# The delta-rule phase of a hybrid block with TensorE's order formed in the source, decays kept in SBUF and one inverse

## The chip, the cores and the metric

The kernel runs on one core of one Trainium2 chip. The metric is the device time of one execution in microseconds (us); of several runs the median counts. Engines are named as in the profile: PE (TensorE; its weight loads are PEld), DVE (VectorE), ACT (ScalarE), POOL (GpSimd) and SP (SyncE, which here only issues DMAs).

## The reference

One layer for 512 tokens of width 1024, float32. Two mixers read the same normalised input through one wide projection `w_in`: a gated delta rule (8 heads, keys of 128, values of 256) and a retention (4 heads of 256 and 512). Their gated outputs pass `w_br`, are mixed, pass `w_out`, and a squared-ReLU MLP follows. The change is in the delta rule, here as the reference has it:

```python
qkv = silu(causal_depthwise_conv(concatenate([qa, ka, va]), conv_a))
qa = l2norm(qa) * A_DK ** -0.5
ka = l2norm(ka)
beta, g = sigmoid(beta_logit), -exp(a_log) * softplus(a_dt + dt_bias)
# in chunks, per head
g_cum = cumsum(g)
decay = exp(where(causal, g_cum[:, None] - g_cum[None, :], -inf))
lower = where(strict, (k * beta) @ k.T * decay, 0)
t_inv = inverse(I + lower)                      # unit lower triangular
u, w = t_inv @ (v * beta), t_inv @ (k * beta * exp(g_cum))
attn = where(causal, q @ k.T * decay, 0)
for each chunk:
    v_new = u - w @ state
    o = (q * exp(g_cum)) @ state + attn @ v_new
    state = state * exp(g_last) + (k * exp(g_last - g_cum)).T @ v_new
oa = rmsnorm(o, norm_a) * silu(za)
```

The reference works in chunks of 64. Both kernels take chunks of 128, four per head, which gives the same sums in another grouping.

## The kernel before

Tokens lie in four tiles of 128, features in tiles of 128. Every weight passes through `weights` (lines 88 to 103): one DMA of 512 KB on SP's queue into one of two buffers `raw`, then a split into a rounded part `whi` (ACT, line 117) and the rest `wlo` (DVE, line 118), three buffers each. Every product is three float32r matmuls, hi x hi, hi x lo and lo x hi: `mm3` (lines 81 to 86), called by `feature_major` and `token_major`. One weight tile feeds 24 matmuls of 512 columns. Results stand in PSUM: four banks `mm` for projections, three `dl` and one `tr` for everything else. Small products and transposes inside the delta rule are plain float32 matmuls.

The stages in time: the start (normalisation, transposition of the input, the first key projection; to about 45 us), the delta rule (to about 430 us), the retention with its products of blocks (`seven`, with block sums that POOL's queue adds in DRAM), the mix, and the MLP.

The order of instructions on each engine comes from a scheduler that reads the program in source order, with priorities: `tc.high_priority(n)` moves a block n places ahead, `tc.keep_in_program_order` fixes an instruction against the others so marked, and `tc.issue_after(x)` puts instructions behind `x` on its own engine. Before, almost all of the delta rule's matmuls were left to the scheduler.

The delta rule before, for groups of four heads (`g4`) and pairs of heads (`g2`):

- `keys` (683): projection, `conv_silu` (630: copy to `c_raw` with a margin of three, one scaled copy on ACT, three multiply-adds on DVE, Tanh on ACT, one closing multiply on DVE, line 646), transposition into `kd`, sums of squares, `rsqrt`. Then per head `decays` and a matrix `mt` of scaled key products (713), and a scaling of `kd` (716).
- `decays` (659): for one head, eight copies of the triangle `tri`, scaled by the two parts of `g` (665, ACT), two matmuls of the constant `later` on them (666), and Exp (668). It is called once per head in `keys` and again in `values_queries`.
- `base_inverse` (720), called for each `g4`: the diagonal blocks of 32x32 of 16 matrices go to DRAM and come back as 64 rows (POOL's queue); 31 elimination steps of two DVE operations each (741, 747); the result goes back through DRAM into `rt` and, for `double_blocks`, into `rn`.
- `double_blocks` (758), four calls of eight matrices: blocks of 32 become blocks of 64 and 128 through four rounds of small matmuls (780, 786/789, 797, 801).
- `values_queries` (804): projections and convolutions of values and queries of a pair, and the masked query-key products `at`.
- `recurrence` (846): per chunk the products with the state (862, 894), with the inverse (871), the state's update (880) and the output (901), with DVE and ACT steps between.
- `gated` (927) projects `za`, and `gate_rows` (600) takes Tanh (604), completes silu (605) and multiplies the rows (607). `gated_features` (609) transposes and splits them into `og`; `ya_partial` (671) multiplies them by `w_br`.

The calls stand at lines 932 to 954; the state of one pair is worked on while the next pair's projections run. Query buffers `qf` are two.

Of the kernel before, what the change touches and what calls it, by code (L numbers as in the profile page):

```python
# [10 lines left out]
F32 = mybir.dt.float32  # L11
# [8 lines left out]
P = 128  # L20
# [7 lines left out]
OFF_GA, OFF_GBR = 12304, 13328  # L28
DFF = 4096


def shape_constants():
# [3 lines left out]
    later = (j[:, None] > j[None, :]).astype(np.float32)  # L36
    c_mat = np.concatenate([ident, tri, later], axis=1)
# [23 lines left out]
def hybrid_block_kernel(ctx: ExitStack, tc: tile.TileContext, a: dict, out: bass.AP):  # L61
# [11 lines left out]
    later_copies = [24]  # L73
    marks = []
# [13 lines left out]
    def weights(src, k0, nk, c0, ncols, keep=None, paced=True):  # L88
# [11 lines left out]
        with ExitStack() as behind:  # L100
            for mark in marks if i < 9 else ():
                behind.enter_context(tc.issue_after(mark.ins))
            return split_weights(raw, n, nk, keep, 200 if i >= 6 else 0)
# [207 lines left out]
    cmat = cp.tile([P, 3 * P], F32, name="cmat")  # L311
# [4 lines left out]
    later = cp.tile([P, P], F32R, name="later")  # L316
# [14 lines left out]
    ghi = cp.tile([P, 4, 8], F32, name="ghi")  # L331
    glo = cp.tile([P, 4, 8], F32, name="glo")
# [30 lines left out]
    rk = pa.tile([P, 32], F32, name="rk")  # L363
    rinv = pa.tile([P, 32], F32, name="rinv")
    br = pa.tile([P, 32], F32, name="br")
    nc.gpsimd.memset(rt, 0.0)

    with tc.tile_pool(name="xp", bufs=2) as xp:
# [64 lines left out]
        def to_features(t, xn, pss):  # L433
            for k in range(8):
                transpose(pss[k % 4][:, k // 4, t % 2 * P : t % 2 * P + P], xn[:, k * P : (k + 1) * P])
# [59 lines left out]
        with tc.issue_after(later_in.ins):  # L495
            nc.gpsimd.dma_start(cmat[:, P : 3 * P], a["c_mat"][:, P : 3 * P])
# [25 lines left out]
        def small_half(th):  # L522
            ts = slice(256 * th, 256 * th + 256)
            for i in range(16):
                nc.tensor.matmul(
                    pba[0:32, ts], ba_w[:, i % 8, 0:32], xs[i // 8][:, i % 8, ts],
                    start=th + i == 0, stop=i == 15, skip_group_check=True,
                )

        pba = psx.tile([P, T], F32, tag="tr", name="pba", bufs=1)  # L530
        small_half(0)
        to_features(2, xn2, pss)
        to_features(3, xn3, pss)
        for k in range(8):
            features(1, k, pss, marks.append)
        small_half(1)
        pv = psx.tile([P, 4, P], F32, tag="dl", name="tr", bufs=3)
        transpose(pv[:, 0, :], vecs_in)
        nc.vector.tensor_copy(vecs, pv[:, 0, 0:18])
        transpose(pv[:, 1, :], conv_in)  # L540
        nc.vector.tensor_scalar(convw, pv[:, 1, :], 0.5, None, ALU.mult)
        with tc.issue_after(marks[-2].ins):
            nc.scalar.copy(later, cmat[:, 2 * P : 3 * P])
# [4 lines left out]
    baT = pa2.tile([32, T], F32, tag="st", name="baT", bufs=2)  # L548
    for i in range(2):
        nc.scalar.copy(baT[:, i * 256 : i * 256 + 256], pba[0:32, i * 256 : i * 256 + 256])  # L550
    pb = psx.tile([P, 4, P], F32, tag="tr", name="tr", bufs=1)
    for c in range(4):
        nc.tensor.transpose(pb[:, c, 0:32], baT[:, c * P : (c + 1) * P], ident[0:32, 0:32])
    scratch = pa2.tile([P, T], F32, tag="vn", name="scratch")
    ba = scratch[:, 0:64].rearrange("p (c h) -> p c h", c=4)

    def small(i):
        return scratch[:, 64 + 32 * i : 96 + 32 * i].rearrange("p (c h) -> p c h", c=4)

    both = scratch[:, 272:400].rearrange("p (c h) -> p c h", c=4)  # L560
    nc.vector.tensor_copy(both, pb[:, :, 0:32])
    nc.vector.tensor_tensor(ba, both[:, :, 0:16], both[:, :, 16:32], ALU.add)
    nc.scalar.activation(beta, ba[:, :, 0:8], AF.Exp, scale=-1.0)
    nc.vector.tensor_scalar(beta, beta, 1.0, None, ALU.add)
    nc.vector.reciprocal(beta, beta)
    z, e, u, lnu, um1, g = (small(i) for i in range(6))
    dt_b = ab[:, 8:16].unsqueeze(1).to_broadcast([P, 4, 8])
    nc.vector.tensor_tensor(z, ba[:, :, 8:16], dt_b, ALU.add)
    nc.vector.scalar_tensor_tensor(e, z, -1.0, z, ALU.mult, ALU.max)
    nc.scalar.activation(e, e, AF.Exp, scale=-1.0)  # L570
    nc.vector.tensor_scalar(u, e, 1.0, None, ALU.add)
    nc.scalar.activation(lnu, u, AF.Ln)
    nc.vector.scalar_tensor_tensor(um1, u, -1.0, e, ALU.add, ALU.subtract)
# [847 lines left out]
```

## Time and profile before

| what | value |
|---|---|
| runs, median of 3 (lowest to highest) | 1362.84 us (1362.74 to 1366.62) |
| span of the profiled execution | 1362.5 us |
| what the median of the runs has over that span | 0.3 us |
| instructions in the span | 17876 |
| granted TensorE clock, mean | 0.999 |
| POOL busy, share of the span | 109.4 us, 8% |
| data moved by DMA | 214.70 MB, mean 158 GB/s |

A row of an engine or of a group gives busy time as the union of its instructions' durations, their count, the mean duration of one in ns, and the idle time of the engine just ahead of them with what ended it. Matmuls overlap, so their durations are longer than the distance between their starts. A row of the windows gives the stretch and its length, then for each engine the busy time and, in brackets, the count, and at the end the granted clock, the share of the DMA engines and GB/s. A row of the waits reads: engine and line that waited, what released it, total us, number of times, longest. A row of the timeline begins with the start in us and the duration of the instruction, or of several alike.

### The profile page before, as it was taken

How to read it: one execution, taken by the hardware profiler on the slowest of the kernel's cores; microseconds unless marked ns; L12 is line 12 of the kernel's file. 1: busy time of each engine (PE TensorE's matmuls, PEld its weight loads, DVE VectorE, ACT ScalarE, POOL GpSimd, SP SyncE). 2: the span in 40 equal slices, each digit the busy share in tenths (PEclk: the TensorE clock that was granted, in tenths of full speed). 3: DMA queues.
4: the chain of work that ended last, by engine and by line, in shares of the span. 5: the costliest groups of instructions: out<-in, count | busy, mean ns of one | idle time of the engine just before them, and what ended most of it. 6: DMA issues, size and time to landing. Idle time of an engine off the chain costs nothing.

```text
span 1362.5 us, 17876 instructions
## 1 busy us (share of the span) xinstructions
PE 1347.0 (99%) x6685; PEld 1110.7 (82%) x6685; DVE 912.8 (67%) x1606; ACT 651.7 (48%) x1204; POOL 109.4 (8%) x161
## 2 busy tenths in 40 slices
PE   9999999999999999999999999999999999999997
PEld 7888787788877888888888888888889888888886
DVE  5799899864665557567477577575775744828535
ACT  5977564624543322453453343343355736436441
POOL 2010310121011002000000100011101100000000
PEclk9999999999999999999999999999999999999999
DMA  5254715379458447775584782488639843625421
GB/s 178 64 154 133 202 43 180 117 153 238 108 124 169 110 147 158 190 240 193 131 255 132 192 263 93 154 217 182 199 117 238 224 154 110 197 95 169 132 86 62
DMA packets 101718, 214.70 MB, mean 158 GB/s; under 512 B 7158, under 2 KB 20624, under 8 KB 101120
## 3 DMA queue, kind: packets, MB, share of 16 engines
q1 hardware_dynamic: 85616, 170.41, 39.1%
q0 software_dynamic: 15280, 42.03, 17.0%
q8 instruction: 52, 0.85, 0.3%
q10 hardware_dynamic: 736, 1.12, 0.2%
q14 instruction: 34, 0.28, 0.1%
HBM read 207.77 MB, written 64.49 MB: 200 GB/s over the span
## 4 chain that ended last, share of the span: by engine, by line
PE 89%; DVE 5%; DMA 2%; ACT 2%; issue 1%; DVEq 0%; ACTq 0%
PE mm L84 18%; PE mm L85 18%; PE mm L86 18%; PE mm L242 10%; PE dl L242 10%; PE tr L323 3%; PE mm L456 2%; DVE wlo L118 1%; PE dl L86 1%; PE dl L85 1%; PE dl L84 1%; PE dl L901 1%; PE dl L871 1%; DVE c_y L642 1%; PE dl L880 1%; PE dl L862 1%
## 5 line engine op out<-in xcount | busy, mean ns | idle before, releaser
L118 DVE TENSOR_TENSOR wlo<-raw,whi 128x1024 fp32r<-128x1024 f32 x245 | 298.8, 1221 | 269.0 <-ACT whi L117 267.7
L117 ACT CAST whi<-raw 128x1024 fp32r<-128x1024 f32 x245 | 257.4, 1052 | 428.9 <-PE mm L85 243.4
L84 PE MATMUL mm<-actT,whi 128*128 128x512 f32 x480 | 190.1, 396 | 0.0
L85 PE MATMUL mm<-actT,whi 128*128 128x512 f32 x480 | 189.9, 396 | 0.0
L86 PE MATMUL mm<-actT,wlo 128*128 128x512 f32 x480 | 189.0, 395 | 0.0
L84 PEld LDWEIGHTS mm<-actT,whi 128*128 128x128 f32 x480 | 90.2, 188 | 18.7 <-ACT c_y L640 0.8
L86 PE MATMUL mm<-hn,wlo 128*128 128x512 f32 (+1 forms) x288 | 105.4, 366 | 0.0
L85 PE MATMUL mm<-hn,whi 128*128 128x512 f32 (+1 forms) x288 | 105.3, 366 | 0.0
L84 PE MATMUL mm<-hn,whi 128*128 128x512 f32 (+1 forms) x288 | 105.3, 366 | 0.0
L86 PEld LDWEIGHTS mm<-actT,wlo 128*128 128x128 f32 x480 | 90.3, 188 | 17.9
L85 PEld LDWEIGHTS mm<-actT,whi 128*128 128x128 f32 x480 | 90.3, 188 | 17.8
L84 PE MATMUL mm<-og,whi 128*128 128x512 f32 x256 | 99.7, 390 | 1.0 <-DVE zz L605 1.0
L85 PE MATMUL mm<-og,whi 128*128 128x512 f32 x256 | 99.6, 389 | 0.0
L86 PE MATMUL mm<-og,wlo 128*128 128x512 f32 x256 | 99.6, 389 | 0.0
L242 PE MATMUL mm<-whi,xsum 128*128 128x512 f32 x256 | 80.8, 389 | 0.0
L642 DVE SCALAR_TENSOR_TENSOR c_y<-c_raw,convw,c_y 128x512 f32<-128x512 f32 x96 | 69.7, 743 | 2.4 <-ACT c_y L640 1.8
L85 PEld LDWEIGHTS mm<-hn,whi 128*128 128x128 f32 x288 | 54.3, 189 | 8.8
L84 PEld LDWEIGHTS mm<-hn,whi 128*128 128x128 f32 x288 | 54.3, 189 | 8.7
L86 PEld LDWEIGHTS mm<-hn,wlo 128*128 128x128 f32 x288 | 54.3, 189 | 8.7
L84 PE MATMUL mm<-whi,actT 128*128 128x512 f32 x152 | 61.1, 402 | 0.1
L242 PE MATMUL dl<-whi,actT 128*128 128x512 f32 x192 | 61.1, 389 | 0.0
L242 PE MATMUL dl<-whi,ffq 128*128 128x512 f32 x192 | 61.0, 389 | 0.0
(345 smaller groups left out, 2608.8 us busy)
## 6 DMA issues: line engine op xcount, KB each, us to landing
raw<-in_w_in_dram SPq DMA_DIRECT2D x101, 512.0 KB, 4.3
raw<-sums SPq DMA_DIRECT2D x56, 512.0 KB, 4.2
raw<-in_w_up_dram SPq DMA_DIRECT2D x36, 512.0 KB, 4.6
sums<-in_w_in_dram SPq DMA_DIRECT2D x32, 512.0 KB, 5.6
sums<-sums POOLq DMA_DIRECT2D x28, 512.0 KB, 7.1
raw<-in_w_down_dram SPq DMA_DIRECT2D x26, 512.0 KB, 3.8
sums<-in_w_down_dram SPq DMA_DIRECT2D x24, 512.0 KB, 7.4
raw<-in_w_br_a_dram SPq DMA_DIRECT2D x16, 512.0 KB, 4.0
```

What stands on the lines that cost most here:

```text
L84: nc.tensor.matmul(ps, lh, rh, start=first, stop=False)
L85: nc.tensor.matmul(ps, lh, rl, start=False, stop=False)
L86: nc.tensor.matmul(ps, ll, rh, start=False, stop=last)
L117: nc.scalar.copy(hi[:, :n], raw[:, :n])
L118: nc.vector.tensor_tensor(lo[:, :n], raw[:, :n], hi[:, :n], ALU.subtract)
L242: m = nc.tensor.matmul(pss[t], lhs[i // 2], rhs[i % 2], start=first and k + i == 0, stop=k + i == 5, skip_group_check=not first,)
L323: nc.tensor.transpose(ps, src, ident)
L456: nc.tensor.matmul(ps[:, ts], ws[w][:, kk, f * P : (f + 1) * P], xs[x][:, k, ts], start=first and kk + i == 0, stop=kk == len(ks) - 1 and ...
L642: nc.vector.scalar_tensor_tensor(y, raw[:, j : j + T], tap(j), y, ALU.mult, ALU.add)
L862: nc.tensor.matmul(ks[:, hh, :], kf[:, h0 + hh, cs], state[:, hh, :], start=True, stop=True)
L871: nc.tensor.matmul(px[:, hh, :], rt[:, nn[hh], :], vx[:, hh, :], start=True, stop=True)
L880: nc.tensor.matmul(pc[:, hh, :], kd[:, nn[hh], :], vn[:, hh, :], start=True, stop=True)
```

## The change

Outside the delta rule two things change: the gate of the retention is one Silu on ACT instead of Tanh and a DVE operation, and a scaling of its `rstd` goes. The constant `later` and its load go. At the start, the transposes of tokens 256 to 511 are interleaved by feature pairs, and half of the second half of the first key product is put ahead of the small projection's second half, all fixed in program order.

The delta rule is written anew:

- **Order.** A class `Clock` runs while the kernel is written, not on the chip. It holds a model of PE's time; each matmul and transpose of the phase goes through it and is fixed in program order. Work is of two kinds. *Chains* (keys, inverse, doubling, recurrence, gates) yield planned delays or names of events. *Fillers* (projections, in pieces of some microseconds) run when no chain is due. Projections for keys, values, queries and `w_br` are cut into pieces of 256 columns, holding two `mm` banks.
- **Decays.** Row sums of `g` go to DRAM once, come back broadcast over the partitions, are masked on POOL, and 32 Exps on ACT with a per-partition bias leave all decays in `dall` (32 x 128 columns of SBUF). The query products are multiplied into the same place.
- **Scalings.** `kd` is not scaled any more; the products with the inverse are copied twice on ACT, with `brd` (decay to the chunk's end included) for the state and with `br` for the output.
- **Convolution.** The three multiply-adds read PSUM, without the copy; Silu on ACT closes it for values and queries (Tanh and a DVE operation still for keys, since every Silu is put behind the last Exp).
- **Inverse.** One `base_inverse` for all 32 matrices on 128 partitions. DVE's own 32x32 transposes take the place of the trips through DRAM. Each operation of a step is cut in two halves. `double_blocks` runs its four rounds over all four groups.
- **Query buffers.** `qf`, `ssq` and `rq` have three buffers, so that the third pair's queries need not wait for the first pair.
- **Gates.** `za` passes Silu straight from PSUM; one DVE multiplication per tile and head follows.

The delays and the lists, as the source has them (lines of the diff, cut):

```diff
+SMALL_US, CONV_US, TOK_US, PK_US, INV_US, DB_US = 10.5, 6.5, 2.5, 2.0, 62.0, 0.5
+VT_US, KS_US, PX_US, PC_US, GATE_US, FEAT_US, INV_PRIO, CONV_PRIO, SMALL_PRIO, KEY_PRIO, DECAY_US, AHEAD, TR_US = 2.5, 2.4, 3.5, 2.4, 11.0, 1.0, 0, 600, 800, 600, 20.0, 700, 2.2
...
+        def run(self, fillers):
...
+                due = [c for c in self.chains if self.ready(c[0]) <= self.now]
+                if due:
+                    self.step(min(due, key=lambda c: self.ready(c[0])))
+                    continue
+                if current is None:
+                    for f in fillers:
+                        if all(self.events.get(n, float("inf")) <= self.now for n in f[1]):
+                            fillers.remove(f)
+                            current = f[0]()
+                            break
...
+            gb = pa2.tile([P, 16, P], F32, tag="vt", name="gb", bufs=2)
+            rows = g_d[16 * g4 : 16 * g4 + 16].rearrange("n t -> (n t)")
+            nc.gpsimd.dma_start(gb.rearrange("p n t -> p (n t)"), rows.partition_broadcast(P))
+            nc.gpsimd.affine_select(
+                gb, gb, pattern=[[0, 16], [1, P]], compare_op=ALU.is_ge, fill=-1e30, base=0, channel_multiplier=-1
+            )
...
+                        nc.scalar.activation(
+                            dall[:, 4 * h + c, :], gb[:, 4 * i + c, :], AF.Exp, bias=neg_g[:, c, h : h + 1]
+                        )
...
-        for j in (2, 1, 0):
-            nc.vector.scalar_tensor_tensor(y, raw[:, j : j + T], tap(j), y, ALU.mult, ALU.add)
-        nc.scalar.activation(th, y, AF.Tanh)
-        nc.vector.scalar_tensor_tensor(dst, th, 1.0, y, ALU.add, ALU.mult)
+            for j in (2, 1, 0):
+                s = 3 - j
+                nc.vector.scalar_tensor_tensor(y[:, s:T], ps[:, 0 : T - s], tap(j), y[:, s:T], ALU.mult, ALU.add)
+            if th is None:
+                with tc.issue_after(exps[-1].ins):
+                    nc.scalar.activation(y, y, AF.Silu, scale=2.0)
...
+                for bs in blocks:
+                    nc.vector.transpose(
+                        mb[bs].rearrange("p (c m) -> p c m", m=32), mt[bs, :, bs].rearrange("p n c -> p c n")
+                    )
+                for j in range(31):
...
+                    cuts = (0, (nr + 1) // 2, nr) if nr > 3 else (0, nr)
...
+            clock.done("inverse", INV_US)
...
+                    qs = chain_bank()
+                    for hh in range(2):
+                        clock.matmul(qs[:, hs[hh], :], qf[:, hh, cs], state[:, hs[hh], :], start=True, stop=True)
+                    yield KS_US - (clock.now - t1)
...
+                    for w, scale in ((vx, brd), (vn, br))[c == 3 :]:
+                        for hh in range(2):
+                            nc.scalar.activation(w[:, hs[hh], :], px[:, hs[hh], :], AF.Copy, scale=scale[:, nn[hh] : nn[hh] + 1])
+                yield PX_US
...
+        clock.run(
+            [
+                (second_keys_filler, ()),
+                (value_filler(0), ()),
+                (query_filler(0), ()),
+                (gate_filler(0), ()),
+                (value_filler(1), ()),
+                (query_filler(1), ()),
+                (ya_filler(0), ("og0", "doubled")),
+                (value_filler(2), ("og0",)),
+                (query_filler(2), ()),
+                (gate_filler(1), ("gate0",)),
+                (ya_filler(1), ("og1",)),
+                (value_filler(3), ("og1",)),
+                (query_filler(3), ("og1",)),
+                (gate_filler(2), ("gate1",)),
+                (ya_filler(2), ("og2",)),
+                (gate_filler(3), ("gate2",)),
+            ]
+        )
```

801 lines of the change are left out of this document (493 added, 308 removed).

## The prediction, written before the result

> **What bounds the kernel now.** I read the page's first lines, then the busy time of each engine by stage (the windows: length, then busy us and count of PE, PEld, DVE, ACT, POOL, then the granted clock), then what PE waited for.
>
> ```profile
> span 1362.5 us, 17876 instructions
> ...
> PE 1347.0 (99%) x6685; PEld 1110.7 (82%) x6685; DVE 912.8 (67%) x1606; ACT 651.7 (48%) x1204; POOL 109.4 (8%) x161
> ```
> ```profile
> 0.00:450.00 450.00, 442.31 (x2531) 358.35 (x2532) 333.57 (x772) 256.97 (x628) 65.26 (x111) 1.00 0.55 142
> 450.00:1300.00 850.00, 849.54 (x3915) 707.43 (x3914) 549.48 (x776) 375.22 (x537) 44.15 (x51) 1.00 0.60 172
> 1300.00:1362.50 62.50, 55.12 (x243) 44.96 (x241) 29.70 (x59) 19.49 (x39) 0.00 (x0) 0.97 0.19 68
> ```
>
> PE is the bound, at full clock. From 450 to 1300 us it misses 0.5 us in 850: the edits there (one DVE operation less per gate tile, no gate scaling) are worth nothing, because PE's own matmuls hide all of it. The last 7.4 us without PE are the final rows, untouched. What can move lies in the first 450 us: start and delta rule, with 7.7 us of PE idle (450.00 - 442.31). There a saving comes either from PE work that goes or from PE waits that go.
>
> What PE work costs is not its busy duration. The timeline of a dense stretch (start, duration, engine, line):
>
> ```profile
> 1150.26 0.39 PE L242 MATMUL dl<-wlo,ffq 128*128 128x512 f32 x1
> 1150.48 0.62 PE L242 MATMUL dl<-whi,ffq 128*128 128x512 f32 x2
> 1150.94 0.39 PE L242 MATMUL dl<-wlo,ffq 128*128 128x512 f32 x1
> ```
>
> Three 512-column matmuls start per 0.68 us, 0.227 us each, though each is shown as 0.39 us. I price PE work by starts. The waits:
>
> ```profile
> PE warm L381 <- DVE warm L370: 1.3, 1, 1.3
> PE dl L880 <- ACT vn L875: 1.2, 1, 1.2
> PE tr L594 <- issue: 1.1, 1, 1.1
> PE mm L84 <- DVE zz L605: 1.0, 1, 1.0
> PE tr L323 <- DVE kf L646: 0.6, 1, 0.6
> PE tr L323 <- DVE vt L607: 0.6, 1, 0.6
> PE tr L406 <- DMA nrow<-in_norm_mix_pre_dram: 0.6, 1, 0.6
> PE dl L666 <- DVE acc L713: 0.5, 1, 0.5
> ```
>
> The first and the seventh belong to the unchanged start. The other six, 5.0 us, are the delta rule's, and four of them end on DVE, which is nearly full in the middle of it:
>
> ```profile
> 80.00:240.00 160.00, 158.29 (x935) 127.16 (x934) 148.80 (x373) 99.81 (x252) 22.10 (x43) 1.00 0.47 145
> ```
>
> **The change, part by part.**
>
> *Decays kept.* Before, each of 8 heads builds its decay twice (keys, queries), each time with two matmuls on `later` and eight scaled copies on ACT:
>
> ```profile
> L666 PE MATMUL dl<-tg,later 128*128 128x512 f32 x32 | 12.1, 433 | 0.6 <-DVE acc L713 0.5
> L665 ACT ACTIVATE tg<-cmat,ghi 128x128 fp32r<-128x128 f32 x64 | 22.5, 403 | 0.3 <-PE dl L666 0.3
> ```
>
> PE saves 32 x 0.227 = **7.3 us**, all on the path. By busy time it would be 12.1. The Trainium skill ("Trainium Kernel Development and Optimization", Performance Expectations) says that matmul busy time is a bad metric because matmuls are pipelined; the starts above agree, so the sum takes 7.3, not 12.1. ACT loses 128 copies, about 45 us of busy time, and gets 32 Exps of 128x128 at about 0.40 (that row is the nearest: same size, a pointer operand), 13 us. That is relief, worth only the waits it removes.
>
> *What the decays wait for instead.* The row sums go to DRAM, come back broadcast over 128 partitions twice (1 MB each) and pass a POOL select of 128x2048.
>
> ```profile
> L836 POOL TENSOR_SCALAR_AFFINE_SELECT at<-at 128x1024 f32<-128x1024 f32 x4 | 7.6, 1892 | 27.2 <-DVE ssq L842 15.6 <-DVE at L832 11.6
> raw<-in_w_in_dram SPq DMA_DIRECT2D x101, 512.0 KB, 4.3
> sums<-in_w_in_dram POOLq DMA_DIRECT2D x16, 512.0 KB, 12.2
> ```
>
> A select takes 2 x 1.9 = 3.8 us, a load between 2 x 4.3 = 8.6 us (SP's row is half the size) and 24 (twice POOL's row). One after the other: store 4.3, load 8.6, select 3.8, load 8.6, select 3.8, 16 Exps 6.4, so 36 us; at POOL's price 74. What can queue behind the Exps on ACT are the `whi` casts, for which PE waits. Three `whi` buffers of 24 matmuls each (24 x 0.227 = 5.45 us a tile) hide 16 us of a standing ACT, and the four tiles of the second keys, 22 us, run before anything needs a decay: 38 us of cover. I take SP's price, nearest in kind (plain DRAM to SBUF), and so **0**; the other end, 74 - 38 = 36 us, works like rival A and is kept there.
>
> *Convolution, keys, gates.* PE's part is unchanged (same transposes, same products). DVE loses the 32 scalings of `kd`, 24 of 32 closing operations of the convolution and one operation of each of 16 gate tiles:
>
> ```profile
> L716 DVE TENSOR_SCALAR kd<-kd,rk,dt 128x128 f32<-128x128 f32 x32 | 11.1, 348 | 0.0
> L646 DVE SCALAR_TENSOR_TENSOR c_y<-c_raw,c_y 128x512 f32<-128x512 f32 x16 | 10.7, 681 | 0.0
> L642 DVE SCALAR_TENSOR_TENSOR c_y<-c_raw,convw,c_y 128x512 f32<-128x512 f32 x96 | 69.7, 743 | 2.4 <-ACT c_y L640 1.8
> L118 DVE TENSOR_TENSOR wlo<-raw,whi 128x1024 fp32r<-128x1024 f32 x52 | 63.4, 1220 | 52.1 <-ACT whi L117 51.7
> L308 DVE SCALAR_TENSOR_TENSOR og<-tr,vecs,og 128x512 fp32r<-128x512 f32 x12 | 8.9, 745 | 4.4 <-ACT og L307 4.4
> ```
>
> 11.1 + 24 x 0.68 + 16 x 0.68 (gates, same size) = 38 us less DVE work. The taps now read PSUM: L308 does so at 745 ns against L642's 743, so nothing is added. The price is that a PSUM bank is held through three taps, about 3 us longer; product pieces of 256 columns that hold two banks of four hide it. Loads of 256 columns have rows of 1 KB instead of 2 KB: SP issues the same 52 tiles, one lands in 4.3 us and feeds 5.45 us of PE, so up to 1.1 us more per load stays hidden; beyond that PE would wait on each.
>
> *Inverse once.* Before: two inverses of 31 steps on 64 partitions.
>
> ```profile
> L741 DVE TENSOR_TENSOR tmp<-mrb 64x255 f32<-64x255 f32 x2 | 0.8, 410 | 0.0
> L741 DVE TENSOR_TENSOR tmp<-mrb 64x31 f32<-64x31 f32 x2 | 0.4, 180 | 0.0
> L748 DVE COPY mrb<-mrb 64x1024 f32<-64x1024 f32 x1 | 1.1, 1131 | 0.0
> ```
> ```profile
> 63.95 0.86 DVE L713 SCALAR_TENSOR_TENSOR acc<-dl,br,dt 128x128 f32<-128x128 f32 x3
> 88.78 0.17 DVE L741 TENSOR_TENSOR tmp<-mrb 64x31 f32<-64x31 f32 x1
> 137.52 0.18 DVE L747 TENSOR_TENSOR mrb<-mrb,tmp 64x31 f32<-64x31 f32 x1
> ```
>
> The shapes give 148 ns + 1.03 ns per element. After: one inverse on 128 partitions, each step halved, 118 operations over 10,912 elements (sum of (31-j)(j+1), twice): 17.5 + 11.2 = 28.7 us. Independent neighbours overlap: three L713 of 344 ns took 0.86 us, 0.26 apart, so 0.08 comes off each: 19 us. The 11 block transposes are shown nowhere; L748 has the size, so 1.1 each and 12 us (0.7 to 2.2 each: 8 to 24). Together 31 us, against 4 x 10.2 = 41 before. The source plans 62 us until PE's doubling of the blocks. In 62 us DVE also has, each less the same 0.08, 11 splits (11 x 1.14 = 13), about six convolution tiles (6 x (3 x 0.66 + 0.60) = 15.5) and one rsqrt chain (some 16 operations of 0.18, 3): 31 + 31 = 62. It just fits. PE's cover: second keys, values 0 and 1, queries 0, 1, 2 and gate 0 need no inverse, 22 tiles x 5.45 = 120 us, 11 of them from the third query buffer. Needed are 22 (second keys' product) + 12 (the last tile's convolution, transposes, sums) + 10 (its 16 scaled products) + 62 = 106 us until the doubling; the 14 left and PE's own 35 us of chain work stand against some 50 us of doubling and first recurrence. That just holds; I take **2 us** of wait. The inverse's trips through DRAM on POOL's queue vanish; PE waited for none of them above. The block sums that POOL adds are no longer ordered behind a POOL instruction; they are read after 450 us only, so 0.
>
> *The formed order.* PE's instructions stand in fixed order; a chain step comes after a planned delay with filler between. The six waits go: the 5.0 us, and 0.16 more each, because a wait begins for the view 0.39 after the last start while PE could start again after 0.227: **6.0 us**. Smaller waits and handovers at the decay matmuls go too: **1.5 us** (32 x 0.046, half of the rise below). In their place 44 handovers of the recurrences (11 a pair of heads) run on planned delays of 2.4 and 3.5 us. Needed after a state product: about 0.4 us to drain, 0.8 on DVE (two halves of a 0.68 us operation), and up to one split of 1.14 in front: 1.2 to 2.4 us. So a few arrive late: **2 us** (0 to 11, at 0.25 each). What a handover itself costs:
>
> ```profile
> 163.53 0.39 PE L84 MATMUL mm<-whi,actT 128*128 128x512 f32 x1
> 163.75 1.02 PE L871 MATMUL dl<-vt,rt 128*128 128x256 f32 x4
> 164.43 0.58 PE L85 MATMUL mm<-wlo,actT 128*128 128x512 f32 x1
> 164.84 0.40 PE L86 MATMUL mm<-whi,actT 128*128 128x512 f32 x1
> ```
>
> After the fp32 piece the next start comes 0.18 late. Pieces this small exist already, so I add 0; 20 more would cost 3.6.
>
> *Start.* Interleaving the key halves fills the 1.1 us wait counted above; the moved transposes wait for the same features: 0 (-2 to +3).
>
> **Sum**: -7.3 - 6.0 - 1.5 + 2 + 2 = **-10.8 us**. The profiled execution spans 1362.5, 0.3 under the runs' median of 1362.84; so 1352.
>
> **Rivals.**
> *A. Inverse late, PE idle behind it (slower).* The one inverse decides when any doubling starts; before, only half of it did. Before's first took from 88.78 to 137.70, 48.9 us, for 20.4 us of its own (62 operations): 2.4 times. If that dilution holds for 31 us it takes 75, and with no overlap (28.7 + 12 = 41) 98: 13 to 36 us over plan, all idle on PE, whose order is fixed. 1352 - 2 + (13 to 36) = 1363 to 1386, say 1372; from 17 us on the kernel is slower. Against it: 38 us less DVE work, and no second inverse.
> *B. Handovers late (no change).* All 44 come 0.25 late, and 20 pieces are added: 1352 - 2 + 11 + 3.6 = 1364.6. For it speaks DVE at 148.8 of 160 us.
> *C. No new waits, start better.* 1352 - 4 - 2 = 1346, near the floor.
> *D. Halving gains nothing.* If none of the 118 operations overlaps, the inverse is 10 us over plan: 1360. The Trainium skill ("VectorE: DVE Perf Modes", The DRAIN you can't avoid) holds that a next operation doesn't start until the pipe is empty, so that few operations are better; L713's spacing of 0.26 us at 344 ns speaks against it here.
> That the change doesn't do what it says: PE's order is pinned, so it fails only by running dry, which is A.
>
> **Chances.** Forecast 0.58 (1348 to 1358), C 0.12, B 0.11, D 0.04, A 0.15. A measurement of this kernel can tell about 0.3% (4 us) from no change. Faster by over that, below 1358.8: forecast and C, 0.70. Within: B, D and the nearest of A, 0.17. Slower, above 1366.9: 0.13. Range: 1343 (C with the start's 3 us more) to 1372 (A's nearer half), which leaves out A's far half and little else.
>
> **What would show it.** No `later` matmul in the trace, decays as 32 Exps. Waits of PE below 450 us sum to 4, not 5.0. Inverse from first to last operation near 62 us; over 75 is A, with one long PE wait before the block products. DVE busy some 45 us less in the first 450. The stretch after the delta rule unchanged. The prediction is wrong if PE waits many times on DVE in the recurrences (B), or on `whi` behind the Exps.

## The result, and the profile after

The changed kernel takes 1379.18 us (median of 6 runs, 1374.88 to 1398.44); the kernel before took 1364.42 in the same session. The ratio is 1.0116, with an interval of 1.0074 to 1.0157: **slower by about 1.2%**, where 1352 was forecast. The profiled execution is one of the longer ones, 27.0 us over before's span. Single executions of the changed kernel differ by up to 23 us: four of the six lie at 1374.88 to 1380.81 with a mean granted clock of 0.992 to 0.996, two at 1391.28 and 1398.44 with 0.984 and 0.978. The longest of the six is left out of the ratio.

The page of the changed kernel, in the same columns as before's:

```profile
span 1389.5 us, 17419 instructions
...
PE 1362.1 (98%) x6655; PEld 1121.5 (81%) x6655; DVE 880.1 (63%) x1491; ACT 609.2 (44%) x1085; POOL 81.1 (6%) x91
...
PEclk9999978999999999999999999999999999999999
```

DVE and ACT are relieved as planned, and PE has 30 instructions less. Yet PE is busy for 15.1 us more. The clock row says why in part: two slices, from 174 to 243 us, stand below 9. The windows:

```profile
0.00:450.00 450.00, 435.43 (x2447) 358.53 (x2448) 306.32 (x649) 203.31 (x466) 37.54 (x41) 0.96 0.55 143
450.00:1300.00 850.00, 844.55 (x3858) 697.16 (x3857) 534.43 (x771) 374.50 (x559) 43.58 (x50) 1.00 0.61 168
```

In the first 450 us PE is idle for 14.6 us (before 7.7), runs 84 matmuls fewer and has a granted clock of 0.96 where it had 1.00. In the next 850 us, where nothing was to change, it is idle for 5.4 us (before 0.5) and runs 57 matmuls fewer. So the time goes in three places: idle PE, half clock, and something behind the delta rule. The waits of PE up to 450 us:

```profile
PE tr L583 <- ACT vt L806: 4.3, 2, 4.0
PE dl L583 <- ACT vt L806: 3.8, 2, 3.5
PE warm L381 <- DVE warm L370: 1.2, 1, 1.2
PE dl L574 <- DVE dall L1024: 1.1, 1, 1.1
PE dl L574 <- DVE mrb L952: 0.8, 2, 0.5
PE tr L406 <- DMA nrow<-in_norm_mix_pre_dram: 0.7, 1, 0.7
```

The six waits of before are gone, and two long ones have come: the value transposes (583) wait 4.0 and 3.5 us for a Silu (806). All waits of that view, with the shorter ones that are not shown, sum to 14.5 us. Of these 2.9 belong to the start, so 11.6 stand against the 4 forecast for the delta rule. The first recurrence has two waits, of 0.6 and 0.3 us (vt 1094, st 1103); from 250 to 450 us, in the other recurrences, the view lists none.

**First loss: the block transposes.** What the Silu waited for is on DVE. Its timeline ahead of the wait that ends at 113.22, and below it ACT's and PE's:

```profile
105.74 2.02 DVE L908 STREAM_TRANSPOSE mrb<-acc 32x1024 f32<-32x1024 f32 x1
107.79 0.75 DVE L803 SCALAR_TENSOR_TENSOR vt<-mm,convw,vt 128x510 f32<-128x510 f32 x1
108.57 1.96 DVE L908 STREAM_TRANSPOSE mrb<-acc 32x1024 f32<-32x1024 f32 x1
110.56 1.22 DVE L120 TENSOR_TENSOR wlo<-raw,whi 128x1024 fp32r<-128x1024 f32 x1
111.71 0.74 DVE L803 SCALAR_TENSOR_TENSOR vt<-mm,convw,vt 128x509 f32<-128x509 f32 x1
```
```profile
112.54 0.63 ACT L806 ACTIVATE vt<-vt 128x512 f32<-128x512 f32 x1 [3.44 <-DVE vt L803]
```
```profile
109.35 0.39 PE L574 MATMUL mm<-actT,wlo 128*128 128x512 f32 x1
113.22 0.83 PE L583 MATMUL dl<-cmat,vt 128*128 128x128 f32 x4 [3.48 <-ACT vt L806]
```

Between the taps of the convolution (803) stand block transposes (908) of 2.0 us each. The last tap starts at 111.71, the Silu at 112.54, and PE, whose order is fixed, stands for 3.48 us. The second wait, of 4.02 us from 159.4 on, has the same form, with block transposes of lines 929 and 933 between the taps. The groups of the inverse on DVE (busy total, mean ns of one):

```profile
L926 DVE TENSOR_TENSOR mrb<-mrb,tmp 128x110 f32<-128x110 f32 (+35 forms) x59 | 12.5, 249 | 0.0
L918 DVE TENSOR_TENSOR tmp<-mrb 128x110 f32<-128x110 f32 (+35 forms) x59 | 12.4, 250 | 0.4
...
L908 DVE STREAM_TRANSPOSE mrb<-acc 32x1024 f32<-32x1024 f32 x4 | 8.0, 2004 | 0.1
L933 DVE STREAM_TRANSPOSE rt<-mrb 32x1024 f32<-32x1024 f32 x4 | 7.9, 1964 | 0.1
...
L929 DVE STREAM_TRANSPOSE rn<-mrb 32x1024 f32<-32x1024 f32 x3 | 7.0, 2327 | 0.1
```

The eleven transposes take 22.9 us (8.0 + 7.9 + 7.0), not 12. The two rows of the 118 operations overlap each other; together they cover 22.1 us, where 19 was forecast. All of it covers 45.0 us of DVE instead of 31. The inverse runs from 98.44 to 174.2, 75.7 us, where the source plans 62.

**Second loss: the clock.** Windows cut at the changes of the granted clock, which stands behind the five engines, third from the end:

```profile
109.70:113.60 3.90, 0.42 (x4) 0.38 (x4) 3.87 (x5) 0.63 (x1) 2.00 (x2) 1.00 0.50 71
113.60:117.00 3.40, 3.40 (x11) 2.73 (x10) 2.28 (x6) 0.78 (x1) 0.00 (x0) 0.50 1.04 204
...
168.20:188.70 20.50, 19.40 (x361) 15.39 (x361) 18.65 (x30) 3.93 (x6) 3.20 (x4) 1.00 0.72 129
188.70:219.40 30.70, 30.70 (x160) 23.13 (x160) 11.35 (x21) 3.98 (x5) 2.31 (x2) 0.50 0.54 121
```

Read it in pairs. After PE's 3.48 us of idleness the clock is halved for 3.4 us; the same follows the other wait, at 164.8. But from 188.7 on it is halved for 30.7 us although PE had been idle for only 1.1 of the 20.5 us ahead (20.50 - 19.40): the doubling of the blocks runs there. Its rows just ahead of the drop and just behind it:

```profile
186.99 1.00 PE L574 MATMUL dl<-rt,mrb 32*32 32x32 f32 x29
...
187.92 0.57 PE L574 MATMUL dl<-mrb,rt 32*32 32x32 f32 x13
188.42 1.03 PE L574 MATMUL mm<-actT,whi 128*128 128x512 f32 x2
189.25 0.63 PE L574 MATMUL mm<-actT,wlo 128*128 128x512 f32 x1
```

A group of 48 matmuls on 32x32 blocks comes first, then three wide matmuls (of 512 columns), then the next group. The wide ones take 0.63 instead of 0.39 from then on. In before no such stretch stands ahead of the last rows.

**Third loss: the spacing after the delta rule.** The matmuls on `hn` in the MLP, in the view of one tile (minimum, median and maximum duration, first and last start); after first, then before, where the same lines are numbered 84 instead of 86:

```profile
L86 PE MATMUL mm<-hn,whi x288: 274/392/405, 1040.5 to 1336.7; 128*128 128x512 f32 x112, 128*128 128x256 f32 x32
```
```profile
L84 PE MATMUL mm<-hn,whi x288: 278/389/396, 1019.0 to 1310.5; 128*128 128x512 f32 x112, 128*128 128x256 f32 x32
```

The same work lasts 296.2 us instead of 291.5, at full clock. Between the starts of neighbouring 512-column matmuls on `hn` lie 233.2 ns in the mean, before 226.8; on `xsum` 232.8 against 226.8; on `actT` 227.7 against 227.6. So it is certain operands that are slow, not PE as a whole, and over the stretch from 530 us on it costs 8 to 9 us.

A small fourth one stands at the seam behind the delta rule. From the waits of the whole execution, and from the chain of waits:

```profile
PE mm L86 <- DVE ro L1270: 2.2, 1, 2.2
```
```profile
512.51 7.40 DMA rope<-in_c_rope_dram
...
521.83 0.61 DVE ro L1270
522.58 0.47 PE mm L86
```

The chain is read from the bottom: PE waited for `ro`, and the chain behind `ro` goes back on DVE to the load of the table `rope`, which takes 7.4 us. The clock halves for 3.4 us right behind the wait (523.2). This one was read, not tested.

### The profile page after: what moved, and what is told of

The parts are those of the page before. It is cut to its first block, busy times and chain, and to the rows that moved or that the text cites. A ratio compares the mean times of both kernels' runs of the same rounds, so it can differ in the third digit from the quotient of the medians.

```text
span 1389.5 us, 17419 instructions
## 1 busy us (share of the span) xinstructions
PE 1362.1 (98%) x6655; PEld 1121.5 (81%) x6655; DVE 880.1 (63%) x1491; ACT 609.2 (44%) x1085; POOL 81.1 (6%) x91
## 3 DMA queue, kind: packets, MB, share of 16 engines
q10 hardware_dynamic: 736, 1.12, 0.2%
## 4 chain that ended last, share of the span: by engine, by line
PE 86%; DVE 6%; ACT 4%; DMA 2%; issue 1%; DVEq 0%; ACTq 0%; POOLq 0%; SPq 0%
PE mm L574 19%; PE mm L86 12%; PE mm L87 12%; PE mm L88 12%; PE mm L244 10%; PE dl L244 9%; PE dl L574 6%; DVE wlo L120 1%; PE tr L583 1%; PE dl L88 1%; PE dl L87 1%; PE dl L86 1%; PE tr L324 1%; DVE vt L803 1%; PE mm L538 1%
## 5 line engine op out<-in xcount | busy, mean ns | idle before, releaser
L574 PE MATMUL mm<-actT,whi 128*128 128x512 f32 x448 | 150.4, 418 | 0.0
L86 PE MATMUL mm<-actT,whi 128*128 128x512 f32 x256 | 101.4, 396 | 1.0 <-ACT g_t L1364 1.0
L87 PE MATMUL mm<-actT,whi 128*128 128x512 f32 x256 | 100.4, 392 | 0.0
L574 PEld LDWEIGHTS mm<-actT,whi 128*128 128x128 f32 x448 | 83.5, 196 | 15.7
L574 PE MATMUL mm<-whi,actT 128*128 128x512 f32 x256 | 88.5, 408 | 0.1
L86 PE MATMUL mm<-og,whi 128*128 128x512 f32 x160 | 63.3, 395 | 2.2 <-DVE ro L1270 2.2
L88 PE MATMUL mm<-og,wlo 128*128 128x512 f32 x160 | 63.0, 394 | 0.0
L87 PE MATMUL mm<-og,whi 128*128 128x512 f32 x160 | 62.9, 393 | 0.0
L574 PE MATMUL mm<-og,whi 128*128 128x512 f32 x192 | 61.9, 404 | 0.0
```

Source lines behind the costliest of these rows:

```text
L86: nc.tensor.matmul(ps, lh, rh, start=first, stop=False)
L87: nc.tensor.matmul(ps, lh, rl, start=False, stop=False)
L88: nc.tensor.matmul(ps, ll, rh, start=False, stop=last)
L574: m = tc.keep_in_program_order(nc.tensor.matmul(*args, **kwargs))
```

## The experiments

Theories at the start: the value transposes come late because DVE's inverse is longer than planned, above all its block transposes (T1 below); and the doubling, a long run of small matmuls with little wide work between, halves the clock (T2). Rival to the first: the planned numbers alone are wrong, and a later plan mends it. Rival to the second: the waits halve the clock, and nothing else. The loss after 530 us had no theory yet. Every run here is set against runs of the kernel before on the same chip, whose medians were 1362.59, 1362.56, 1361.94 and 1363.64 in the four sessions.

**Doubling spread.** Two planned us between the groups of the doubling instead of half a us, which puts two to three times as much wide work between them.

```diff
-SMALL_US, CONV_US, TOK_US, PK_US, INV_US, DB_US = 10.5, 6.5, 2.5, 2.0, 62.0, 0.5
+SMALL_US, CONV_US, TOK_US, PK_US, INV_US, DB_US = 10.5, 6.5, 2.5, 2.0, 62.0, 2.0
```

> Only the planned delay between steps of the block doubling goes from 0.5 to 2.0 us, so that nine large matmuls instead of three stand between two groups of small ones. Theory T1 (late DVE work: the block transposes of 2.0 to 2.3 us hold up the convolutions, PE waits on Silu, and the waits of 3.5 and 4.0 us are what drops the clock): both long waits stay, a half-clock stretch of many us stays with them, time 1375 to 1385. Theory T2 (thin filler: the clock drops because small matmuls with little between them use too little of the array): no half-clock stretch in the doubling, only the 3.4 us after each long wait; mean clock 0.996 or more, time 1367 to 1372, but PE may run short of filler in the first recurrence, up to 5 us of waits.

Measured: 1379.31 (1377.35 to 1380.80), ratio 1.0122 [1.0107, 1.0137]. The stretch of 30.7 us is gone, as T2 had it; half clock stands at 114.0 (3.4 us), 161.8 and 216.4 (6.8 each). The first two stand at the waits for the Silu, which stay (3.8 and 3.5). The third follows the last of the small matmuls, 48 of 64x64 in a row and then a wait of 0.6 us. The time is T1's, and T2's 1367 to 1372 is missed: the median does not move, and the executions lie within 3.5 us of each other. Four of the changed kernel's six executions have no lower clock than these, so its median holds little of the long stretch.

**A later plan.** The inverse announced at 78 us, and 5 us more between convolution and transposition of the first values.

```diff
-            clock.done("inverse", INV_US)
+            clock.done("inverse", 78.0)
...
-            yield clock.vector(2.1, 0.9) + CONV_US
+            yield clock.vector(2.1, 0.9) + CONV_US + (5.0 if g2 < 2 else 0.0)
```

> Only planned delays: the inverse 78 instead of 62 us, and 5 us more between a value tile's convolution and its transposition for the first two pairs. T1: the two waits on Silu (7.5 us) and those at the first doubling steps go, and with them the short clock drops: 1362 to 1368, unless the filler now runs out before the inverse is done. T2: the waits go, but the doubling keeps its thin filler and its half clock: 1368 to 1380.

Measured: 1382.51 (1378.19 to 1389.03), ratio 1.0161 [1.0124, 1.0199]. T1's 1362 to 1368 is missed. The waits move:

```profile
PE mm L574 <- DVE vt L803: 3.7, 1, 3.7
...
PE mm L86 <- ACT keep L119: 3.3, 1, 3.3
PE mm L574 <- DVE mrb L926: 1.8, 1, 1.8
```

Now a projection waits 3.7 us for the taps of an earlier tile, which still hold its bank. DVE has the same work to do, so a plan that tells the truth only chooses where PE stands. The rival falls.

**No block transposes.** Trips through DRAM on POOL's queue in place of the eleven transposes, with one DVE copy (1.12 us) for the transposed result.

```diff
-                for bs in blocks:
-                    nc.vector.transpose(
-                        mb[bs].rearrange("p (c m) -> p c m", m=32), mt[bs, :, bs].rearrange("p n c -> p c n")
-                    )
+                for b, bs in enumerate(blocks):
+                    nc.gpsimd.dma_start(scr_m[b].rearrange("n (m c) -> m n c", m=32), mt[bs, :, bs])
+                nc.gpsimd.dma_start(mb, scr_m.rearrange("b n e -> (b n) e"))
...
+                nc.gpsimd.dma_start(scr_r.rearrange("b n e -> (b n) e"), rb)
+                nc.vector.tensor_copy(mb3, rb3.transpose([0, 2, 1]))
+                nc.gpsimd.dma_start(scr_t.rearrange("b n e -> (b n) e"), mb)
...
-                    nc.vector.transpose(rt[blocks[b], :, blocks[b]].rearrange("p n c -> p c n"), rb3[blocks[b]])
+                    nc.gpsimd.dma_start(rt[blocks[b], :, blocks[b]], scr_t[b].rearrange("n (m c) -> m n c", m=32))
```

> The eleven block transposes on DVE are replaced by trips through DRAM on POOL's queue, as before the change (one copy of 128x1024 stays on DVE). T1: DVE loses 23 us between the taps, the waits on Silu shrink below 1 us each, the inverse is done about 12 + 35 + 10 us after the key products: time 1360 to 1367 if the clock follows the waits. T2: waits shrink, the doubling still halves the clock in some runs: 1366 to 1378, with spans that differ by over 5 us between runs.

Measured: 1367.70 (1361.87 to 1382.82), ratio 1.0036 [1.0006, 1.0066], 11.5 us less than the changed kernel. Behind the start's 45 us and up to 500 PE's longest wait is now this:

```profile
PE dl L574 <- DVE dall L1025: 1.1, 1, 1.1
```

The Silu is not among them, and no half clock follows at 113. But in the doubling:

```profile
150.00:176.50 26.50, 26.50 (x397) 21.40 (x396) 19.24 (x34) 5.59 (x8) 6.83 (x9) 1.00 0.99 227
176.50:207.20 30.70, 30.70 (x160) 23.13 (x161) 10.75 (x16) 3.99 (x5) 7.19 (x7) 0.50 0.81 129
```

PE is busy for 26.50 of the 26.50 us ahead of the drop: no wait is there to halve the clock.

**Both.**

> Both: trips through DRAM and 2.0 us between doubling steps. T1: same as with the trips alone, within 3 us. T2: 7 to 15 us less than with the trips alone, mean clock 0.998, 1352 to 1360.

Measured: 1365.42 (1362.89 to 1370.77), ratio 1.0019 [1.0004, 1.0033]: 2.3 us under the trips alone, where T2 forecast 7 to 15. The ten executions all have a granted clock of 0.996 or more, where three of ten without the spread had 0.981 to 0.987; it is these three that the spread mends, and they weigh little in a median. A half-clock stretch of 3.4 us is left at 206, behind the last of the small matmuls. The long waits and the long stretch are gone, and the kernel is still not faster than before: the third loss is left, with `hn` at 233.3 ns.

**The layout.** The change drops 1152 bytes a partition of constants (`later` 512, a third of `cmat` 512, two tiles of 128 for one) and the small tile `sp_h` of 128, so every tile allocated behind them lies elsewhere. First all of it put back, as tiles that nothing uses:

```diff
     neg_g = cp.tile([P, 4, 8], F32, name="neg_g")
+    pad_c = cp.tile([P, 288], F32, name="pad_c")
+    pad_s = sm.tile([P, 32], F32, name="pad_s", bufs=1)
```

> The changed kernel with two tiles that nothing uses: 1152 bytes a partition behind `neg_g` and 128 bytes ahead of the small tiles, so that every tile allocated behind them (weights, activations, `xsum`, `hn`, `ffq`) lies at the byte at which the kernel before has it. No instruction differs. Theory L (the place of the operands in SBUF sets the spacing of the matmuls): the matmuls on `hn` after 530 us go back from 233 ns apart to 227, those on `xsum` and `ffq` too, and the time falls by 8 to 9 us to about 1370. Rival O (the spacing is something that the delta phase leaves behind, or the program as a whole): the spacing stays at 233 and the time at 1379.

Measured: 1369.72 (1365.60 to 1389.72), ratio 1.0038 [1.0024, 1.0052]: 9.5 us less than the changed kernel, by two tiles without an instruction. `hn` 226.8 ns, `xsum` 226.5. The waits for the Silu are unchanged (4.1 and 3.5).

The same in the version with both remedies:

> All three remedies in the changed kernel: the eleven block transposes as DRAM trips, the doubling spread among four times as much other work, and the layout of before. Theory L: 1365.4 of the two remedies without the layout less 8 to 9, about 1357, faster than both kernels, with 227 ns on `hn`. Rival O: 1365.4.

Measured: 1357.43 (1355.69 to 1358.12), ratio 0.9956 [0.9943, 0.9969]: faster than both kernels. And the other way round, the kernel before with the changed kernel's places for `hn`, `xsum` and `ffq`:

```diff
-    cmat = cp.tile([P, 3 * P], F32, name="cmat")
-    ident, tri = cmat[:, 0:P], cmat[:, P : 2 * P]
+    ident = cp.tile([P, P], F32, name="ident")
...
-    ghi = cp.tile([P, 4, 8], F32, name="ghi")
-    glo = cp.tile([P, 4, 8], F32, name="glo")
...
+    tri_later = pa.tile([P, 2 * P], F32, name="tri_later")
+    tri = tri_later[:, 0:P]
+    ghi = pa.tile([P, 4, 8], F32, name="ghi")
+    glo = pa.tile([P, 4, 8], F32, name="glo")
```

> The kernel before, with 1280 bytes a partition of its constants (the two triangles, `ghi`, `glo`) moved to the pool of the delta phase, so that `hn`, `xsum`, `ffq` and what lies between lie at the bytes at which the changed kernel has them. Same instructions, same order. Theory L: the matmuls on `hn` go from 227 ns to 233, and the time from 1362.6 to about 1371, without any part of the change. Rival O: 227 ns and 1362.6.

Measured: 1363.16, ratio 0.9999 [0.9990, 1.0008], `hn` 226.9 ns. **Missed**: at the very bytes at which the changed kernel is slow, before is not. The second shift, with `later` moved too:

> The same with 1792 bytes moved (`later` too), 512 bytes further than the changed kernel's layout. Theory L, if it is one bad place: 227 ns and about 1362.6 again. Theory L, if the kernel before had hit a good place: slower than before, by up to 9 us, with some spacing between 227 and 238 ns. Rival O: 1362.6.

Measured: 1362.22, ratio 0.9996 [0.9987, 1.0004], `hn` 226.6 ns. So it is not the place of `hn`, although padding cures it. What the shifted versions keep and the changed kernel doesn't is the distance from the weights: `whi` and `wlo` lie ahead of the small tiles, `hn`, `xsum` and the rest behind, and of what lies between only `sp_h` has changed. With `sp_h` the distance from `whi` to `hn` is 83,968 bytes, 82 times 1024; without it 83,840. `actT`, whose matmuls are not slower, lies ahead of the small tiles too. A new theory, then: the distance between the two operands of a matmul, modulo some power of two. Its tests:

```diff
     neg_g = cp.tile([P, 4, 8], F32, name="neg_g")
+    pad_s = sm.tile([P, 32], F32, name="pad_s", bufs=1)
```

> The changed kernel with the 128 unused bytes ahead of the small tiles alone, without the 1152 of the constants. The weights then stay where the changed kernel has them (`whi` at byte 43,936), and `hn` moves by 128 to 127,904; between them lie 83,968 bytes, a whole number of 512 (82 times 1024), as in the kernel before, its two shifted versions and the padded ones. In the changed kernel it is 128 less. Theory D (the distance of the moving operand from the weights, modulo some power of two, sets the spacing): 227 ns on `hn` and about 1370, as with the whole padding. Theory L (the byte itself): 233 ns and 1379.

Measured: 1368.61 (1365.65 to 1386.86), ratio 1.0060 [1.0030, 1.0090], `hn` 226.7 ns. 128 bytes do what 1280 did. The kernel before without them:

```diff
-    ghr = sm.tile([P, 4, 8], F32R, tag="sp_h", name="sp_h", bufs=1)
+    ghr = cp.tile([P, 4, 8], F32R, name="sp_h")
```

> The kernel before with one small tile of 128 bytes a partition, `sp_h`, moved from the small tiles to the constants: `hn` stays at byte 129,056, the weights move up by 128 to 45,216, and the distance is 83,840, that of the changed kernel. Theory D: 233 ns on `hn`, and 8 to 9 us more, about 1371. Theory L: 227 ns and 1362.6, since `hn`, `xsum` and `ffq` lie where they did.

Measured: 1370.46 (1369.15 to 1372.34), ratio 1.0055 [1.0043, 1.0067], at a clock of 0.998 to 0.999: 8.5 us slower by the move of one tile of 128 bytes. Its row for `hn`:

```profile
L84 PE MATMUL mm<-hn,whi x288: 273/392/399, 1018.3 to 1314.6; 128*128 128x512 f32 x112, 128*128 128x256 f32 x32
```

A median of 392 ns and 296.3 us from first to last start, as in the changed kernel. The version with the 1152 bytes but without the 128, and one with 384:

```diff
+    pad_c = cp.tile([P, 288], F32, name="pad_c")
...
+    pad_s = sm.tile([P, 96], F32, name="pad_s", bufs=1)
```

(the first line is the one version, on the trips and the spread doubling, the second the other).

> The changed kernel with the trips and the spread doubling and the 1152 unused bytes in the constants, without the 128: weights where before has them (45,088), `hn` at 128,928, distance 83,840. Theory D: 233 ns and 1365.4, as without any padding, although nearly all of the padding is there. Theory L: by the byte, anything between; 1357.4 if what matters is the weights' place.

Measured: 1365.35 (1362.77 to 1371.34), ratio 1.0024 [1.0009, 1.0038], `hn` 233.2 ns: no gain from nine tenths of the padding.

> The trips and the spread doubling with 384 unused bytes ahead of the small tiles: distance 84,224, 256 more than a whole number of 512. Theory D with a period of 256: 227 ns and 1357.4. Theory D with a period of 512 or more: above 227 ns, and 1360 to 1368. Theory L gives no number.

Measured: 1355.90 (1353.80 to 1356.24), ratio 0.9944 [0.9932, 0.9957]; `hn`:

```profile
L86 PE MATMUL mm<-hn,whi x288: 278/389/397, 1008.5 to 1300.0; 128*128 128x512 f32 x112, 128*128 128x256 f32 x32
```

Back at 389 ns and 291.5 us. A distance of a whole number of 256 bytes is good, one that is 128 off is not; other remainders were not tried.

These runs move whole groups of tiles, so they leave open whether the second operand counts or another tile that moves with it. One execution of the changed kernel answers that, with the places that the built kernel gives to each tile. `ffq` lies in several buffers. On `whi`, its matmuls from buffers at a whole number of 256 bytes start 227.0 ns apart (288 pairs of neighbours), those from the buffer that is 128 off 232.9 ns (45 pairs). `actT` with `keep`, weights held in tiles of their own from 1001 to 1040 us, starts 226.9 ns apart at a whole number (45 pairs) and 232.6 ns at 128 off (65 pairs). So it is the distance between the two operands of the matmul itself.

**The doubling's density.** On this last version, with no late Silu and the layout mended, the planned time between the groups of the doubling is 0.5 us (the thin version), 0 (the bare one), and 4 us (2 in the version above).

> The last kernel (trips, spread doubling, 384 unused bytes) with the doubling in the changed kernel's own spacing again, three wide matmuls between the groups of small ones. Theory C (a run of small matmuls with little wide work between halves the clock by itself, in some executions): most executions within 3 us of 1356, some 10 to 20 us above, with a half-clock stretch inside the doubling. Rival W (only waits halve the clock): 1356 throughout, since the trips have taken the waits away.

Measured: 1366.85 (1354.50 to 1376.86). The ratio is 1.0004 [0.9976, 1.0033]. Four of ten executions lie at 1354.5 to 1360.5 with a clock of 0.995 or more, six at 1366.5 to 1376.9 with 0.980 to 0.986.

> The same with nothing planned between the groups of the doubling, which makes the run of small matmuls denser. Theory C: a half-clock stretch in the doubling in nearly every execution, 10 to 20 us above 1356, and the granted clock at or under 0.99. Rival W: only the handovers between the groups, a few us, and a clock as in the spread version.

Measured: 1366.75 (1364.70 to 1372.96), ratio 1.0031 [1.0014, 1.0048]: all ten executions with a clock of 0.984 to 0.987.

> The same with four planned us between the groups in place of two. Theory C and rival W: 1356 within 2 us, as the clock is whole with 2 us already; slower only if the recurrences behind the doubling then start late.

Measured: 1354.07 (1352.88 to 1356.41), ratio 0.9931 [0.9916, 0.9947], the best version, all with 0.996 or more.

The same 30.7 us of time in the thin, the bare and the 2 us version (in this order; the second from 162.3 on, where its doubling runs):

```profile
176.20:206.90 30.70, 30.70 (x167) 23.24 (x164) 10.23 (x16) 3.71 (x5) 7.20 (x7) 0.50 0.77 127
```
```profile
162.30:193.00 30.70, 30.62 (x363) 28.32 (x361) 17.05 (x30) 2.20 (x5) 3.72 (x4) 0.50 0.83 144
```
```profile
176.20:206.90 30.70, 30.11 (x358) 25.07 (x357) 20.74 (x32) 9.49 (x25) 7.19 (x7) 1.00 0.91 184
```

PE is busy nearly throughout in all three, and at half clock in two. Since the ends of matmuls are modelled, the starts are the better witness: in the 12.3 us ahead of the bare version's drop no start comes more than 0.10 us later than the distance that its shape has at full clock, and all that is late sums to 0.3 us. In the 26.2 us ahead of the thin version's drop it is again at most 0.11 us at a time, 2.6 us in all. The denser the small matmuls, the more executions lose the clock: none of four at 4 and at 2 us, six of ten at 0.5, ten of ten at 0 (one execution of each was profiled; the others are counted by their mean clock). The rival, that only waits do it, falls. What it is in the small matmuls that counts was not tried. The bare version also has a wait of 3.7 us (584 for 821), but behind the doubling. What follows a wait is a second, smaller thing: 3.4 to 6.8 us of half clock at or behind each wait of 3.5 us or more for a value, in the changed kernel, the spread one and the two padded ones alike, and nothing at that place in the versions with trips.

## Why the prediction was wrong

**The step that failed first is "Inverse once": "L748 has the size, so 1.1 each and 12 us (0.7 to 2.2 each: 8 to 24)".** A transposition of 32x1024 is not priced like a copy of 64x1024; it took 1.96 to 2.33 us, at the upper bound and over it, 22.9 us in all. With the 118 operations at 22.1 instead of 19, the inverse's own work was 45 us where the prediction had 31 in a plan that "just fits". Removing the transposes, for trips and a copy of 1.12 us, ended the long waits and gave 11.5 us. The bound of 24 was named; at it, the prediction's own sum (31 + 31 against 62) would have been 43 + 31, and the forecast should have gone to the rival.

**Rival A had the size and not the place.** Its 1363 to 1386 contains the result, and its 75 us is the measured 75.7. But PE did not stand ahead of the block products: their waits (`mrb`, 952) sum to 0.8 us. It stood at 109 and at 159 us, at value transposes whose taps had to share DVE with the inverse. The taps stood in the prediction's budget of DVE, but the sum had PE wait for the inverse alone. What is late behind a long block of work on one engine is whatever else that engine serves meanwhile.

**The clock was no term of the sum at all.** "PE is the bound, at full clock" is true of before. The formed order gathers the doubling into one stretch, and that made PE's own rate fall. This is worth about 11 us in the median between the thin and the 2 us version (1366.85 and 1355.90, in two sessions whose medians of before differ by 1.7). In the changed kernel it is the difference between single executions, and little of its median.

**"The edits there are worth nothing" (after 450 us) failed by what is no edit there.** The list of the change's parts had the constant `later` and its load as a saving and `sp_h` not at all; nobody prices 128 bytes. It cost 8.5 us in before and 9.5 in after, at a distance of half a millisecond from the code that changed. And the seam cost 2 to 3 us of waits.

**What was right.** The decays: every matmul of the execution priced by the distance between starts that its shape has at full clock sums to some 7 us less than before, where 32 x 0.227 = 7.3 was forecast; the decays are 32 Exps,

```profile
L766 ACT ACTIVATE dall<-gb,neg_g 128x128 f32<-128x128 f32 x32 | 10.9, 422 | 0.0
```

and their trip through DRAM shows in no wait of PE. (The 1.1 us on `dall`, line 1024, is for the query products that DVE multiplies into the same tile.) The six waits went. The handovers of the recurrences, 2 us forecast, show as waits of 0.3 to 0.6 that sum to about 1; rival B is wrong. DVE was to be busy 45 us less in the first 450; it is 27 (333.57 to 306.32), and the inverse's 14 us over its estimate are most of the difference. Rival D is wrong: 118 operations of 250 ns would be 29.5 us end to end and cover 22.1. Neighbours overlap by 0.08 us, as the prediction priced them, except where the next step's multiplication follows a subtraction (0.02 in the mean). The section of the Trainium skill that D cites ("VectorE: DVE Perf Modes", The DRAIN you can't avoid) also says that a next operation that is not held starts earlier. These rows agree with that. Rival C, no new waits, was not seen.

With the three losses undone, the windows of the best version come near to what the prediction described:

```profile
0.00:450.00 450.00, 442.52 (x2576) 369.49 (x2577) 297.48 (x667) 214.40 (x492) 48.69 (x55) 1.00 0.59 154
450.00:1300.00 850.00, 844.07 (x3875) 701.79 (x3874) 531.20 (x756) 377.32 (x555) 43.58 (x50) 1.00 0.60 169
```

The clock is full, and the time is 9.6 us less than before in its session (1363.64 to 1354.07), against the forecast's 10.8. PE is idle for 7.5 us in the first 450; the waits listed there sum to 7.4, and 4.4 of them are the delta rule's, where 4 was forecast. Of the 5.9 us idle behind 450, 2.7 are the seam's. That the total comes so near is in part luck: the forecast had no idle PE behind 450 us, and it did not price the trips and the wider spacing of this version. Undone one behind the other, the losses are 11.5 us (trips), 2.3 (spread) and 8.0 (layout), from 1379.18 to 1357.43 in the medians of three sessions. The clock's 11 us above cannot be put in place of the 2.3, because the long stretch came in two of six executions of the changed kernel and in three of ten with the trips, but in six of ten of the thin version.

## What to carry to other kernels

Price an operation by its kind before its size, and where the bound of an unknown price breaks a plan that "just fits", forecast at the bound. When a source forms PE's order, look for runs of small matmuls and mix wide work between them (here two planned us between groups of 48), since here one stretch of 30.7 us at half clock cost this PE-bound kernel some 10 us. After any change of what is allocated, compare the distance between the starts of the same matmuls far from the edit: if only some operands are slower, look at the layout before looking at the code.

## What the runs showed of the hardware that was not expected

- **Small matmuls halve the clock without idleness.** Groups of 32x32 and 64x64 matmuls with three wide ones between: half clock for 30.7 us with PE busy for 30.70, and a clock that fits this in six of ten executions; in all ten with nothing planned between. In the thin and the bare version the starts show at most 0.11 us lost at a time ahead of it. The steps are 3.4 us or several of them (30.7 is nine). The Trainium skill ("TensorE: Matmul & The Clock Gate", Part 1: The HAM clock gate) tells of a window of about 3.4 us of activity and of idle windows that halve the clock; the steps of 3.4 us agree, also behind the waits, and the case without an idle window goes beyond it.
- **The distance between a matmul's two operands in SBUF sets its spacing.** 226.6 to 226.9 ns between 512-column matmuls on `hn` at distances from `whi` of 83,968 and 84,224 bytes (ten of the seventeen kernels), 233.2 to 233.3 at 83,840 (the other seven); 2.8%. Why is open.
- **DVE's transposition of fp32 blocks is slow for its size.** 32x1024 in 1.96 to 2.33 us, where one copy of 128x1024 with the same exchange of strides took 1.12.
